# Second mixer block in float16 halves, the third block's pool groups projected in the fourth, scale sums by one product

## The chip, the cores and the metric

The kernel runs on one core of a Trainium2 chip. The metric is the device time of one execution in microseconds; three executions of the kernel before took 2219.76, 2223.6 and 2225.92 us, the median is 2223.6 us. The profile is of one more execution.

## The reference

The kernel computes one streaming step of a hybrid encoder layer for 2048 prompt tokens and 64 decode tokens, D_MODEL 1024, all inputs in float32:

```python
def hybrid_layer(x, conv_prev, s_prev, pool_prev, pos0, chunk, ...):
    h = rmsnorm(x, norm1_w)
    proj = h @ w_in                               # 1024 -> 2568 columns
    qkv_pre, z, a, b, u_pool = ...                # columns of proj
    qkv, conv_new = causal_short_conv(qkv_pre, conv_prev, conv_w)
    ...                                           # l2norm of q, k; gates g, beta from a, b
    o, s_new = gated_delta_chunked(q, k, v, g, beta, s_prev, chunk)
    o = rmsnorm(o, onorm_w) * silu(z)             # 4 heads of 128 columns
    o_pool, pool_new = multiscale_pool(u_pool, pool_prev, pos0, pool_w, pool_scale)
    x = x + concatenate([o_delta, o_pool]) @ w_out
    h = rmsnorm(x, norm2_w)
    x = x + (silu(h @ w_gate) * (h @ w_up)) @ w_down
```

The gated delta rule is a recurrence over chunks of tokens, four heads side by side. The pool group has four groups of 128 columns, each with its trailing mean of 2, 4, 8 or 16 frames.

## The kernel before

**Tiling.** The 2112 tokens are worked off as four mixer blocks: block 0 has 576 (with the 64 decode tokens), blocks 1 to 3 have 512 each. After them the FFN runs over three groups of 704 tokens by a Strassen scheme in float16 halves. In a mixer block, `project` makes 21 tiles of 128 columns: tile 0 holds the gate columns, tiles 1 to 16 the four heads (q, k, v, z for each), tiles 17 to 20 the pool groups. To keep float32 precision each factor is cut into a high and a low half, and a tile takes three products for each of its eight k (high x high, high x low, low x high), 24 matmuls; tile 0 takes 16. That is 496 matmuls for a block of 512 tokens. The output projection (`out_proj`) has 8 x 24 = 192 for each block.

**Two kinds of halves.** `J16` gives the first block that works in float16: a block with `B.f16 = j >= J16` has float16 halves, which need scales that are powers of two, from the sums of squares of a weight tile. The others have float32r halves (`wsplit`). Before, J16 is 2:
- block 0 loads each raw tile of `w_in` as two pieces (`wrp`, 256 KB each), splits it on ScalarE and VectorE, squares it on ScalarE for its scale (sums in `psq`), and stores the float32r halves to DRAM (`wsd`, in the profile `wnd`);
- block 1 loads the halves back from there;
- block 2 loads the raw tiles again, converts them to float16 halves (`convert`, `split16`: ScalarE scales and rounds the high half, VectorE takes the rest) and stores them (`w16`, in the profile `wn`);
- block 3 loads those.

The output weights go the same way, one block later: block 0's output projection runs in block 1 and prepares float32r halves, block 1's runs in block 2 and loads them back (`wod`), block 2's and 3's run behind block 3 with float16 halves, whose scales `convert` makes from squares of its own (`two_squares`, `wcwout`).

**Scales.** `scale_of` turns n columns of partial sums into one scale: VectorE copies the columns to bfloat16, TensorE multiplies each column by a constant matrix (n products of one column, summed in PSUM), and `half_power` makes a power of two from the bits in three VectorE operations. It is used for FFN weights (`ws` with 4 columns, `wd` with 2), for the FFN's activations (`ec` with 8), and for `wcwout`. `win_scales` makes the scales of all 21 tiles of `w_in` at once, at the start of block 1; `out_scale` makes those of the mixer's outputs, in block 3.

**Order.** A list `plan` names the weight tiles in the order of their use; `prep` prepares them three ahead of use. `PRE_AT` names the places in it where sums of FFN weights are prepared early. The mixer's recurrence (`Chain` objects, moved on by `pump` inside the matmul loops) runs between the wide matmuls of the projections. All operations are recorded first. A planner (`Machine.issue`) then plays the order of each engine with costs of its own, in windows of operations and with random variations, and keeps the play in which TensorE loses least. `emit` prints the winning order, so that nearly every instruction has the line of that loop, L374 before and L375 after. SP issues all DMAs.

**The third block** (`B.kept`, j = 2) is a special case: its output projection doesn't run in the next block but at the very end. Its heads' and pools' results wait in DRAM (`od`), and are loaded and split to halves behind block 3 (`od{k}`). Its pool groups (`pools(B)`) are projected at the end of block 2; the fourth block projects its own behind its last head (`LASTPOOLS`).

Of the kernel before, what the change touches and what calls it, by code (L numbers as in the profile page):

```python
# [11 lines left out]
BF16 = mybir.dt.bfloat16  # L12
# [41 lines left out]
LASTPOOLS = {3: ((0,), (1,), (2, 3))}  # L54
# [10 lines left out]
class Machine:  # L65
# [126 lines left out]
    def issue(self):  # L192
# [4 lines left out]
        while len(self.out) < len(ops):  # L197
# [3 lines left out]
            for i in range(PLAYS):  # L201
# [6 lines left out]
                self.play(stop + AFTER)  # L208
# [103 lines left out]
    def play(self, stop):  # L312

        wait, ready, total = self.wait, self.ready, self.total
        while len(self.out) < total and self.front < stop:
# [28 lines left out]
            self.out.append(op)  # L344
            for nm in op.tiles:
# [116 lines left out]
def hybrid_kernel(ctx, tc, a, o):  # L462
# [69 lines left out]
    ctx.enter_context(tc.manual_schedule())  # L532
    tc.nc.scalar.preload_act_table_set("natural_log_exp_and_others")
# [80 lines left out]
    def half_power(out, x):  # L614

        ts(out, x, TINY, None, ALU.add)
        bits = out.bitcast(mybir.dt.int32)
        ts(bits, bits, 1, 0x7F800000, ALU.logical_shift_right, ALU.bitwise_and)
        ts(bits, bits, -1.0, float(189 << 23), ALU.mult, ALU.add)

    def scale_of(out, squares, n, top, ps, tag="sqb"):

        cols = (cpool if tag == "sqb" else wq["pool"]).tile([P, 8], BF16, tag=tag, name=f"{tag}{machine.n}", bufs=2)[:, :n]
# [39 lines left out]
    for j in range(NBLK):  # L663
# [3 lines left out]
        if j < NBLK - 1:  # L667
            plan += win[:at] + ([("wout", m) for m in range(KT)] if j else []) + win[at:]
        else:
            plan += win[:1]  # L670
            for h in range(NH):
                plan += win[1 + 4 * h : 5 + 4 * h] + [win[17 + g] for gs in LASTPOOLS.get(h, ()) for g in gs]
        plan[base:] = with_pres(j, plan[base:])
    assert not pres
    plan += [("hw", "wout", m) for m in range(KT)]
    LASTO = ([(m, p) for ms in (range(6), range(6, KT)) for p in (1, 0) for m in ms])
    plan += [("wl", m, p) for m, p in LASTO]

# [41 lines left out]
    def prep():  # L720
# [13 lines left out]
        elif key in stored and key[0] in wsd:  # L734
            parts = []
            for i in range(2):
                t = wtiles(f"p{i}")[1]()
                nc.sync.dma_start(out=flat(t), in_=wsd[key[0]][key[1], i])
                parts.append(t)
# [3 lines left out]
        elif key[0] in ("win", "wout"):  # L743
            parts = []
            for i in range(2):
# [91 lines left out]
    def convert(key, t):  # L837

        _, nm, m = key
        raws = []  # L840
# [18 lines left out]

    def win_scales():  # L860

        cols = gp.tile([P, 2, 21], BF16, tag="cols", name="cols")
        nc.vector.tensor_copy(cols, psq)
        ps = psp.tile([P, 512], F32, tag="mm", name="wscales", bufs=PSM)[:, :21]
        for i in range(2):
            mm(ps, parts_b[2.0**15], cols[:, i], start=i == 0, stop=i == 1)
# [787 lines left out]

    def pools(B, groups=((0,), (1,), (2, 3))):
# [5 lines left out]
    def out_proj(B):  # L1661
        acts = [(k, B.o[k]) for k in (4, 5, 6, 7, 0, 1, 2, 3)]

        src = stream_x(a["xT"], "xc", B.t0, "xc")
        for ms in ((0, 1), *((m,) for m in range(2, KT))) if B.kept else ((m,) for m in range(KT)):
            ws = [weights("hw", "wout", m) if B.f16 else weights("wout", m) for m in ms]
            for m in ms if B.f16 else ():
# [576 lines left out]
```

## Time and profile before

| | |
|---|---|
| median of three executions | 2223.6 us |
| lowest and highest | 2219.76 and 2225.92 us |
| the profiled execution | 2219.34 us, span 2217.6 us |
| DMA | 466.41 MB, mean 210 GB/s |
| chain that ended last | PE 30%, DVE 1%, all others 0% (the rest isn't named) |

The profiled execution took 2219.34 us, of which 2217.6 us are the span from its first instruction to its last. Times in rows count from the start of that span. A row that groups instructions gives the line, engine, operation, tiles (out <- in, buffer numbers left out), shapes and count, then the busy time in us, the mean ns of one, and the idle time of the engine ahead of them with what ended it. Row names: `pp` is the PSUM tile of a projection, `pz` that of an output projection, `wsp` a tile of weight halves, `wrp` a raw weight tile, `h` and `op` the halves of the activations; names with `_p` and `_s` belong to the recurrence of the prompt and of the decode tokens. Matmuls are pipelined, so their durations overlap, and the mean duration of one is longer than the time until the next may start. A row of the timeline gives start, length, engine, line, operation, tiles and count of instructions that follow each other.

The first matmul waits 8.7 us for its weights; blocks 0 to 3 then start at 8.7, 209.2, 438.1 and 648.0 us, the last output projections at 824.6, the FFN at 928.2.

### The profile page before, as it was taken

Reading aid. Unit: us, or ns where it says so; the run is one execution under the profiler, and the core shown is the slowest. Engines: PE = TensorE matmul, PEld = TensorE weight load, DVE = VectorE, ACT = ScalarE, POOL = GpSimd, SP = SyncE. Lnnn points to the kernel's source line nnn. Section 1 sums busy time; section 2 is a strip of 40 time slices with the busy share of each in tenths; the row PEclk is TensorE's granted clock in tenths of the full one; section 3 lists DMA queues with packets and bytes.
Section 4 is the critical chain, followed back from the end, with each engine's and each line's share of the span. In section 5 each row is a group of like instructions: output and inputs, shape, how many; then the busy total and the mean of one; then the engine's idle time right before and its main releaser. Section 6 shows DMA issues by size and latency. Waiting matters only on the chain. (4 is left out here: it accounts for less than half of the span.)

```text
span 2217.6 us, 41377 instructions
## 1 busy us (share of the span) xinstructions
PE 2178.4 (98%) x14785; PEld 1535.4 (69%) x14785; DVE 1597.9 (72%) x3361; ACT 1364.6 (62%) x3235; POOL 652.4 (29%) x783
## 2 busy tenths in 40 slices
PE   8999999999999999999999999999999999999998
PEld 7999898767656666468666676666666566666667
DVE  7888785797779798688899977656543845445447
ACT  7998776787778996587666846732333343312414
POOL 3424342435335563021321117532101421100102
PEclk9999999999999999999999999999999999999999
DMA  7765577566664458996785668978545656444442
GB/s 280 245 213 172 163 269 268 174 211 230 212 216 145 143 157 285 303 333 238 232 295 205 216 204 288 341 244 265 156 143 158 201 186 220 154 145 151 140 140 72
DMA packets 222270, 466.41 MB, mean 210 GB/s; under 512 B 27504, under 2 KB 88944, under 8 KB 222064
## 3 DMA queue, kind: packets, MB, share of 16 engines
q1 hardware_dynamic: 221488, 463.06, 63.5%
q8 instruction: 115, 1.88, 0.3%
q14 instruction: 91, 0.75, 0.1%
q10 hardware_dynamic: 576, 0.72, 0.1%
HBM read 320.26 MB, written 143.43 MB: 209 GB/s over the span
## 5 line engine op out<-in xcount | busy, mean ns | idle before, releaser
L374 PE MATMUL pp<-h,wsp 128*128 128x288 f32 (+2 forms) x2480 | 517.9, 354 | 11.7 <-DVE wsp L374 10.2
L374 PEld LDWEIGHTS <-wsd 128*128 128x128 f16 x2352 | 229.7, 98 | 127.5 <-issue 6.2
L374 PEld LDWEIGHTS pp<-h,wsp 128*128 128x128 f32 x1488 | 226.8, 191 | 27.0 <-ACT wsp L374 8.7
L374 PE MATMUL dx<-hq,wsd 128*128 128x352 f16 x1232 | 233.0, 314 | 1.8 <-DVE y L374 1.5
L374 PEld LDWEIGHTS <-ws11S 128*128 128x128 f16 x1584 | 153.7, 98 | 83.0 <-ACT ws11S L374 1.5
L374 PEld LDWEIGHTS <-wsS 128*128 128x128 f16 x1584 | 154.1, 98 | 82.3 <-issue 2.0
L374 PEld LDWEIGHTS <-wsS3S 128*128 128x128 f16 x1584 | 154.3, 98 | 81.2 <-issue 0.5
L374 POOL TENSOR_TENSOR q<-hr,hr 128x352 f32<-128x352 f32 x52 | 53.9, 1036 | 444.6 <-DVE hr L374 391.2
L374 PEld LDWEIGHTS <-wsp 128*128 128x128 f16 x1184 | 109.1, 98 | 106.8 <-issue 2.7
L374 DVE SCALAR_TENSOR_TENSOR y<-dx,es,y 128x352 f32<-128x352 f32 x240 | 136.0, 580 | 63.7 <-PE dx L374 62.8
L374 ACT COPY g<-px 128x352 f32<-128x352 f32 x132 | 58.4, 443 | 190.3 <-PE px L374 188.9
L374 ACT ACTIVATE hr<-g,pscale 128x352 f32<-128x352 f32 x132 | 76.6, 586 | 143.3 <-DVE g L374 143.0
L374 PE MATMUL pz<-op,wsp 128*128 128x288 f32 (+2 forms) x768 | 158.6, 347 | 0.0
L374 PE MATMUL px<-hA,ws11S 128*128 128x352 f16 x792 | 139.2, 313 | 0.3 <-DVE ws11S L374 0.2
L374 PE MATMUL py<-hA,ws11S 128*128 128x352 f16 x792 | 137.9, 313 | 0.9 <-ACT ws11S L374 0.9
L374 PE MATMUL pz<-hA,wsS 128*128 128x352 f16 x792 | 136.5, 312 | 0.0
L374 PE MATMUL py<-hA,wsS3S 128*128 128x352 f16 x792 | 134.4, 312 | 0.3 <-ACT u L374 0.3
L374 PE MATMUL px<-hA,wsS 128*128 128x352 f16 x792 | 130.8, 312 | 1.4 <-ACT g L374 1.3
L374 PE MATMUL px<-hB,ws 128*128 128x352 f16 x792 | 130.2, 312 | 1.1 <-DVE u L374 0.9
L374 PE MATMUL px<-hA,wsS3S 128*128 128x352 f16 x792 | 130.6, 313 | 0.0
L374 PE MATMUL dy<-hq,wsd 128*128 128x352 f16 x672 | 124.9, 313 | 3.0 <-ACT hq L374 2.3
L374 ACT CAST TV_p<-pt_p 128x512 f16<-128x512 f32 x192 | 110.0, 586 | 23.3 <-PE pt_p L374 20.2
(797 smaller groups left out, 4838.6 us busy)
## 6 DMA issues: line engine op xcount, KB each, us to landing
ws11S<-g SPq DMA_DIRECT2D x44, 512.0 KB, 3.8
wsS<-g SPq DMA_DIRECT2D x44, 512.0 KB, 3.6
wsS3S<-g SPq DMA_DIRECT2D x44, 512.0 KB, 3.6
wrp<-in_win_dram SPq DMA_DIRECT2D x84, 256.0 KB, 3.5
wnd<-wsp SPq DMA_DIRECT2D x42, 512.0 KB, 4.9
wsp<-wnd SPq DMA_DIRECT2D x42, 512.0 KB, 4.0
wsd<-dn SPq DMA_DIRECT2D x40, 512.0 KB, 3.6
xd<-x2d SPq DMA_DIRECT2D x96, 176.0 KB, 3.9
```

The costliest lines, as they stand in the source:

```text
L374: getattr(getattr(self.nc, op.eng), name)(*args, **kw)
```

## The change

It has four parts.

1. **J16 from 2 to 1.** Block 1 and its output projection (which runs in block 2) work in float16 halves. `convert` now runs for block 1's tiles, in blocks 0 and 1; blocks 2 and 3 load the float16 halves. The float32r stores and reloads (`wnd`, `wod`) are gone. Block 0's output projection stays in float32r. `win_scales` runs ahead of the first conversion instead of at the start of block 1, and `out_scale` in block 1 instead of block 3.
2. **Scales of the output weights** come from squares that are taken when block 0's float32r halves of them are prepared (16 pieces, in block 1), all eight at once (`wout_scales`, with `tile_sums`), instead of from `two_squares` and `scale_of` in each `convert`. Their inverse is multiplied with the output scale once.
3. **The third block's pool groups** are projected in block 3, behind the fourth block's heads, with the same weight tiles as the fourth block's own (`pools_of(prev, B)`): for each group 24 matmuls of block 2, then 24 of block 3. So the last output projection of the third block takes its k in the order 0 to 7, heads first.
4. **`scale_of`** sums the n columns on VectorE (`tensor_reduce`) and makes one product of one column. `half_power` has two operations instead of three.

Beside these, `es` gets three buffers, `PRE_AT` has other places, and the planner gives up a play that is already worse than the best (which changes no winner).

```diff
-LASTPOOLS = {3: ((0,), (1,), (2, 3))}
...
     def half_power(out, x):
-        ts(out, x, TINY, None, ALU.add)
         bits = out.bitcast(mybir.dt.int32)
-        ts(bits, bits, 1, 0x7F800000, ALU.logical_shift_right, ALU.bitwise_and)
+        ts(bits, x.bitcast(mybir.dt.int32), 1, 0x7F800000, ALU.logical_shift_right, ALU.bitwise_and)
         ts(bits, bits, -1.0, float(189 << 23), ALU.mult, ALU.add)
...
     def scale_of(out, squares, n, top, ps, tag="sqb"):
-        nc.vector.tensor_copy(cols, squares[:, :n])
-        for i in range(n):
-            mm(ps[:, :1], parts_b[top], cols[:, i : i + 1], start=i == 0, stop=i == n - 1)
+        nc.vector.tensor_reduce(out=cols, in_=squares[:, :n], op=ALU.add, axis=mybir.AxisListType.X)
+        mm(ps[:, :1], parts_b[top], cols, start=True, stop=True)
         half_power(out, ps[:, :1])
...
-            plan += win[:at] + ([("wout", m) for m in range(KT)] if j else []) + win[at:]
+            if j == NBLK - 2:
+                win = win[:17]
+            plan += win[:at] + ([("hw", "wout", m) if j > J16 else ("wout", m) for m in range(KT)] if j else []) + win[at:]
...
-        elif key in stored and key[0] in wsd:
-            parts = []
-            for i in range(2):
-                t = wtiles(f"p{i}")[1]()
-                nc.sync.dma_start(out=flat(t), in_=wsd[key[0]][key[1], i])
-                parts.append(t)
...
-                if key[0] == "win":
+                if len(key) == 2:
                     act(raw, raw, AF.Square, accum_out=psq[:, i, key[1] : key[1] + 1])
                 parts.append(t)
-            if len(key) == 2:
-                due.append((key, [(wsd[key[0]][key[1], i], t) for i, t in enumerate(parts)]))
...
     def convert(key, t):
         _, nm, m = key
+        if m == 0:
+            (win_scales if nm == "win" else wout_scales)()
...
-        if nm == "win":
-            scale = pscale[:, 0, m : m + 1]
-        else:
-            sq = two_squares(f"c{nm}{m}", *raws, t[:, 1, 1].bitcast(BF16))
-            scale, inv = (pscale[:, j, 21 + m : 22 + m] for j in range(2))
-            scale_of(scale, sq, 2, 2.0**15, psp.tile([P, 512], F32, tag="mm", name=f"wc{nm}{m}", bufs=PSM))
-            nc.vector.reciprocal(inv, scale)
+        m0 = 0 if nm == "win" else 21
+        scale = pscale[:, 0, m0 + m : m0 + m + 1]
...
+    def wout_scales():
+        half_power(pscale[:, 0, 21:], tile_sums(KT, "wo"))
+        nc.vector.reciprocal(oinv, pscale[:, 0, 21:])
+        ts(oinv, oinv, oscale[:, 5:], None, ALU.mult)
...
+    def pools_of(*blocks):
+        for g in range(4):
+            w = weights("hw", "win", 17 + g)
+            for B in blocks:
+                ps = psmm(f"pp{B.j}_{17 + g}_0")
+                for k in range(KT):
+                    one_k(B, 17 + g, w[k // 4], ps[:, : B.NB], k, slice(0, B.NB))
+                    pump()
+                B.pools.append(Chain(pool_group(B, g, [ps])))
...
-        acts = [(k, B.o[k]) for k in (4, 5, 6, 7, 0, 1, 2, 3)]
+        acts = [(k, B.o[k]) for k in (range(KT) if B.kept else (4, 5, 6, 7, 0, 1, 2, 3))]
...
-        if j == NBLK - 1:
+        if j == J16:
             out_scale()
-        if j == 1:
-            win_scales()
...
-            if nxt is None and h in LASTPOOLS:
-                pools(B, LASTPOOLS[h])
+            if nxt is None and h == NH - 1:
+                pools_of(prev, B)
...
         if nxt is not None:
-            pools(B)
+            if not B.kept:
+                pools(B)
...
-PRE_AT = {1:(4,8,12,16,20),2:(4,7,10,13,16,19),3:(3,6,9,12,15)}
+PRE_AT = {1: (4, 8, 12, 16, 20), 2: (4, 7, 10, 13, 14, 16), 3: (3, 7, 11), 4: (3, 5)}
...
-J16 = 2
+J16 = 1
```

What the planner makes of it stands in the order of the engines. In its names the number behind the letters is the block, and the next ones tell the tile: `pp1_9_0` is tile 9 of block 1, `wsp` its weights, `pz0_7` the output projection of block 0, and `pk`, `po`, `Gam`, `vn` belong to the recurrence.

TensorE in block 1, tile 9, before:

```order
L374 MATMUL pp1_9_0_1273<-h0_1_839,wsp0_53_1206 128x512 x6
L374 MATMUL pp1_9_0_1273<-h1_1_840,wsp1_53_1207 128x512
L374 MATMUL pk1_p1_1_1_1315<-vn1_p1_1_1_1327,ktl_p1_1_1_1084 128x128
L374 MATMUL po_p1_1__1274<-Gam_p1_1_1_1135,vn1_p1_1_1_1327 128x128
L374 MATMUL pp1_9_0_1273<-h1_1_840,wsp1_53_1207 128x512 x2
L374 MATMUL pz0_7_288_1259<-op0_0_219,wsp0_51_1176 128x288 x12
```

The same place now:

```order
L375 MATMUL pk0_p1_1_0_1296<-rhs0_p1_1_0_1297,X_p1_1_0_1245 128x128
L375 MATMUL po_p1_1__1293<-Qd_p1_1_0_1096,Sp_207 128x128
L375 LDWEIGHTS onesb_101
L375 MATMUL wd4_2_1085<-sqb3464_1086,onesb_101 128x1
L375 MATMUL pz0_7_288_1278<-op0_0_219,wsp0_51_1192 128x288 x7
L375 LDWEIGHTS wsp_53_1222
L375 MATMUL pp1_9_0_1292<-h_1_844,wsp_53_1222 128x512
L375 LDWEIGHTS Wh_p1_1_1_1175
L375 MATMUL pf_p1_1_1_1274<-TV06_p1_1_1_1265,Wh_p1_1_1_1175 128x128
```

A float32r matmul stands in the list without a weight load; each float16 one has an instruction of its own for it ahead. The scale product `wd` stands alone where it was one of two.

ScalarE at the seam of blocks 0 and 1, from the operation that ends `win_scales`' sums (`wscales` before), before:

```order
L374 ACTIVATE psq_107,oscale_106<-wscales_895 128x4 x2
L374 CAST Wh_p0_3_1_753<-Gst_p0_3_1_745 128x256
L374 CAST Wh_s0_755<-Gst_s0_733 128x256
L374 ACTIVATE vn0_p0_2_1_758<-pk0_p0_2_1_756,kn_p0_2_1_533 128x128
L374 CAST h0_1_839<-xb0_576_841 128x512
```

The same place now, where the sums are called `wiscales`:

```order
L375 ACTIVATE psq_107,oscale_106<-wiscales_736 128x4 x2
L375 CAST hi_p0_2__822<-osq_p0_2__805 128x512
L375 CAST TV11_p0_3_1_780<-pt1_p0_3_1_787 128x512
L375 ACTIVATE wsp_22_734<-wrp0_22_737,pscale_105 128x4x64 x2
L375 ACTIVATE qsq_p0_3__935<-Yqk0_3_559 128x512
L375 ACTIVATE wsp_22_734<-wrp1_22_738,pscale_105 128x4x64
L375 ACTIVATE osq_p0_2__805<-os_p0_2__821,qeps_99 128x512
L375 CAST TV11_s0_789<-pt1_s0_796 128x512
```

The conversions of block 1's tile 0 (`wsp_22`) stand between operations of block 0's recurrence now. ScalarE's conversions of 128x512 from `wrp` to float16 numbered 0, 11, 33 and 16 in blocks 0 to 3, and number 10, 34, 16 and 0 now.

ScalarE where the third block's first pool groups are read out of PSUM (`pe2_0`, `pe2_1`), at the end of block 2 before:

```order
L374 ACTIVATE pe2_0_2074<-pp2_17_0_2057,pscale_105 128x512
L374 CAST TV06_p2_2_1_2122<-pt6_p2_2_1_2129 128x512
L374 ACTIVATE wsp_99_2032<-wrp1_99_2034,pscale_105 128x512
L374 ACTIVATE E1_2_3_2051<-E1_2_3_2051 128x512
L374 ACTIVATE TV1F_p2_2_1_2137<-TV32F_p2_2_1_2136 128x256
L374 ACTIVATE pe2_1_2103<-pp2_18_0_2073,pscale_105 128x512
```

Now these stand at the end of block 3, each followed by the fourth block's own group (`pe3_0`):

```order
L375 ACTIVATE pe2_0_2669<-pp2_17_0_2644,pscale_105 128x512
L375 ACTIVATE Yvz3_3_2540<-ext3_11_2590,consts_95 128x512
L375 CAST TV11_p3_2_0_2601<-pt1_p3_2_0_2610 128x512
L375 ACTIVATE YtF_p3_1_0_2606<-px_p3_1_0_2605 128x256
L375 ACTIVATE YtF_p3_1_1_2609<-px_p3_1_1_2608 128x256
L375 ACTIVATE E1_3_3_2640<-Yqk3_3_2539 128x512
L375 ACTIVATE E1_3_3_2640<-E1_3_3_2640,onec_98 128x512
L375 ACTIVATE E1_3_3_2640<-E1_3_3_2640 128x512
L375 CAST TV02_p3_2_0_2624<-pt2_p3_2_0_2631 128x512
L375 ACTIVATE pe3_0_2703<-pp3_17_0_2660,pscale_105 128x512
```

The recurrence around them is now that of the fourth block (`p3`) instead of the third (`p2`), and no conversion of weights stands between them.

More of the change, by code (lines that the diff above doesn't have):

```diff
@@ L344, in play @@
             self.out.append(op)
+            if limit is not None and self.free["tensor"] - self.work >= limit:
+                return
             for nm in op.tiles:
@@ L532, in hybrid_kernel @@
     ctx.enter_context(tc.manual_schedule())
+    ctx.enter_context(tc.nc.allow_low_precision(reason="sums of squares that choose a power of two"))
     tc.nc.scalar.preload_act_table_set("natural_log_exp_and_others")
@@ L858, in convert, with tile_sums, win_scales @@
         due.append((key, [(w16[nm][m], t.rearrange("p i q n -> p (i q n)"))]))
[L860 to L864, printed above, removed]
+    def tile_sums(n, name):
+        cols = gp.tile([P, 2, 21], BF16, tag="cols", name=f"cols{name}")[:, :, :n]
+        nc.vector.tensor_copy(cols, psq[:, :, :n])
+        ps = psp.tile([P, 512], F32, tag="mm", name=f"{name}scales", bufs=PSM)[:, :n]
         for i in range(2):
             mm(ps, parts_b[2.0**15], cols[:, i], start=i == 0, stop=i == 1)
+        return ps
+    def wout_scales():
+        half_power(pscale[:, 0, 21:], tile_sums(KT, "wo"))
+        nc.vector.reciprocal(oinv, pscale[:, 0, 21:])
+        ts(oinv, oinv, oscale[:, 5:], None, ALU.mult)
+    def win_scales():
+        ps = tile_sums(21, "wi")
         for i, lo, step in ((0, 4, 4), (1, 17, 1)):
@@ L1666, in out_proj @@
             ws = [weights("hw", "wout", m) if B.f16 else weights("wout", m) for m in ms]
-            for m in ms if B.f16 else ():
-                ts(oinv[:, m : m + 1], oinv[:, m : m + 1], oscale[:, 5:], None, ALU.mult)
             for lo, n in B.subs:
@@ L1812, in hybrid_kernel @@
     machine.boost = ODB
-    for k in (4, 5, 6, 7, 0, 1, 2, 3):
+    for k in range(KT):
         t = wpool.tile([P, 512], F32, tag="xc", name=f"od{k}", bufs=XBUFS["xc"])
```

18 lines of the change are left out of this document (9 added, 9 removed).

## The prediction

> **What bounds the kernel now.** I first read the totals on the page (busy time, share of the span and instructions of each engine), then the busy time by stage. The six stretches start where each stage's first projection matmuls stand: blocks 0, 1, 2 and 3, the last output projections, and the FFN. A row gives the stretch, its length, busy time (instructions) of PE, PEld, DVE, ACT and POOL, the granted clock, the DMA engines' share and GB/s.
>
> ```profile
> PE 2178.4 (98%) x14785; PEld 1535.4 (69%) x14785; DVE 1597.9 (72%) x3361; ACT 1364.6 (62%) x3235; POOL 652.4 (29%) x783
> ```
> ```profile
> 8.70:209.20 200.50, 197.17 (x1566) 185.56 (x1567) 175.25 (x390) 180.81 (x495) 78.22 (x109) 1.00 0.67 224
> 209.20:438.10 228.90, 228.02 (x1558) 195.80 (x1557) 165.54 (x364) 168.66 (x408) 80.84 (x114) 1.00 0.67 221
> 438.10:648.00 209.90, 206.77 (x1275) 133.96 (x1275) 176.33 (x357) 171.95 (x409) 84.21 (x110) 1.00 0.66 217
> 648.00:824.60 176.60, 170.84 (x1171) 105.29 (x1170) 147.97 (x340) 155.09 (x394) 98.80 (x132) 1.00 0.51 156
> 824.60:928.20 103.60, 103.38 (x616) 56.84 (x614) 77.50 (x175) 61.19 (x144) 25.60 (x26) 1.00 0.84 278
> 928.20:2217.60 1289.40, 1272.18 (x8608) 857.91 (x8607) 851.85 (x1722) 622.05 (x1380) 282.23 (x286) 1.00 0.63 207
> ```
>
> TensorE is busy 98% of the span and its clock is granted in full in every stage. The length of a stretch less TensorE's busy time is its idle time: 3.3 us in block 0, 0.9 in block 1, 3.1 in block 2, 5.8 in block 3, 0.2 in the tail and 17 in the FFN. So the time is TensorE's queue, and an edit is worth what it takes out of that queue, less any new idle time. ScalarE and VectorE are loaded to 70 to 90% in blocks 0 to 2, which is where they could become late.
>
> **Term A: 688 matmuls go from float32r to float16.** These are the second block's 496 wide projection matmuls and the 192 wide ones of its output projection.
>
> ```profile
> L374 PE MATMUL pp<-h,wsp 128*128 128x512 f16 x992 | 237.1, 379 | 2.0 <-DVE wsp L374 1.5 <-DVE h L374 0.3
> L374 PE MATMUL pp<-h,wsp 128*128 128x512 f32 x496 | 128.9, 401 | 0.0
> L374 PE MATMUL pz<-op,wsp 128*128 128x512 f32 x192 | 52.4, 406 | 0.0
> L374 PE MATMUL pz<-op,wsp 128*128 128x512 f16 x192 | 46.5, 379 | 0.0
> ```
>
> The mean durations overlap each other in the pipeline, so I take busy time per matmul: 128.9/496 = 260 ns against 237.1/992 = 239 ns, and 52.4/192 = 273 against 46.5/192 = 242. By these rows the change is worth 496 x 0.021 + 192 x 0.031 = 10.4 + 5.9 = 16.3 us. That is the upper bound, because a busy time also holds the pipeline's fill and drain at each switch to another operation. What one matmul adds to the queue is read from the timeline, from one row's start to the next row's:
>
> ```profile
> 363.50 15.67 PE L374 MATMUL pp<-h,wsp 128*128 128x512 f32 x68
> 379.01 0.60 PE L374 MATMUL ptk_p<-consts,Yqk 128*128 128x128 f32 x4
> ...
> 635.11 2.97 PE L374 MATMUL pp<-h,wsp 128*128 128x512 f16 x13
> 637.92 0.22 PE L374 MATMUL px_p<-TV_p,TV1F_p 128*128 128x128 f16 x1
> ...
> 398.04 0.28 PE L374 MATMUL py_p<-TV_p,Wh_p 128*128 128x128 f16 x2
> 398.12 2.09 PE L374 MATMUL pp<-h,wsp 128*128 128x512 f32 x8
> 400.05 0.23 PE L374 MATMUL py_p<-TV_p,Wh_p 128*128 128x128 f16 x1
> 400.12 0.28 PE L374 MATMUL pt_p<-Yt_p,TV_p 128*128 128x128 f16 x2
> 400.23 0.28 PE L374 MATMUL pt_p<-TV_p,Yt_p 128*128 128x128 f16 x2
> ```
>
> 68 float32r matmuls take 379.01 - 363.50 = 15.51 us, 228 ns each; 13 float16 ones 2.81 us, 216 ns each. In long runs the step is 12 ns, and 688 x 12 ns = 8.3 us, the lower bound. The third piece shows why it is more: a run of 8 that follows a narrow float16 pair takes 1.93 us, 0.20 us over 8 x 0.216, where the long run's price gives 0.10. The pair ahead of it takes 0.08 us; the pair behind it takes 0.11 (400.12 to 400.23), so 0.03 is given back, and each such switch costs some 0.075 us that float16 doesn't pay. I count 57 runs of this kind; the first and the last:
>
> ```profile
> 210.55 1.41 PE L374 MATMUL pp<-h,wsp 128*128 128x512 f32 x5
> 211.80 0.38 PE L374 MATMUL po_p__703<-Gam_p,vn_p 128*128 128x128 f32 x2
> ...
> 567.31 1.17 PE L374 MATMUL pz<-op,wsp 128*128 128x512 f32 x4
> 568.32 0.40 PE L374 MATMUL os_p__1908<-hi_p__1909,ones 128*128 128x512 f32 x1
> ```
>
> Their excess over 216 ns is 1.25 - 1.08 = 0.17 and 1.01 - 0.86 = 0.15 us, of the same size. So 8.3 + 57 x 0.075 = **12.6 us**, between 8.3 and 16.3.
>
> A float16 matmul has a weight load of its own, and the other rows to weigh are these:
>
> ```profile
> L374 PEld LDWEIGHTS pp<-h,wsp 128*128 128x128 f32 x1488 | 226.8, 191 | 27.0 <-ACT wsp L374 8.7 <-DVE h L374 1.1 <-issue 0.9
> L374 PEld LDWEIGHTS <-wsp 128*128 128x128 f16 x1184 | 109.1, 98 | 106.8 <-issue 2.7 <-DVE wsp L374 2.0
> ```
>
> Both kinds load 128 columns per matmul, 191 ns in float32r and 98 ns in float16, and both are shorter than the matmul that they can hide behind. The Trainium skill, "TensorE: Matmul & The Clock Gate", section "The mechanism", says that a weight load overlaps running matmuls only where it targets other rows of the array. All loads here cover 128 rows, so by that rule 688 x 98 ns = 67 us would stand open after the change; the 13 float16 matmuls at 216 ns, each with its load, contradict it.
>
> **Term B: 199 products of one column go.** The scales of power-of-two halves were made by n products of one column each, now by one sum on VectorE and one product. By the instruction lists of the two kernels there were 112 (`ec`), 88 (`ws`), 44 (`wd`) and 16 (`wcwout`), of which 15, 22, 22 and 0 stay, and two products of 8 columns come in: 260 - 59 - 2 = 199.
>
> ```profile
> L374 PE MATMUL ec<-sqe,onesb 128*128 128x1 bf16 x112 | 4.9, 164 | 0.0
> 1071.56 0.34 PE L374 MATMUL ec<-sqe,onesb 128*128 128x1 bf16 x8
> 1071.76 1.35 PE L374 MATMUL py<-hA,wsS3S 128*128 128x352 f16 x8
> ```
>
> Eight of them hold the queue for 0.20 us, 25 ns each: **5.0 us**. By busy time it is 0.34/8 = 42 ns, so 8.5 us at most, and nothing at least, where the next wide matmul would have waited anyway. The same page's section "Wait — 56ns, not 53.3ns?" gives some 62 ns for a small matmul when its decoding is done in software, by which these would be 12 us; the 25 ns of the row are the floor that it gives for decoding in hardware. VectorE has one operation for another here and one less in each scale, off the path.
>
> **What lies beside other work, at 0.** The conversions to float16 move forward by a block.
>
> ```profile
> L374 ACT ACTIVATE wsp<-wrp,pscale 128x512 f16<-128x512 f32 x56 | 39.0, 719 | 5.1 <-PE pp L374 2.7 <-DVE pscale L374 1.7 <-PE pz L374 0.4
> L374 ACT ACTIVATE wrp<-wrp 128x512 f32<-128x512 f32 x42 | 26.5, 632 | 0.9 <-DVE wsp L374 0.9
> L374 ACT ACTIVATION_READ_ACCUMULATOR wrp<-wrp 128x1 f32 x42 | 8.3, 197 | 0.0
> L374 DVE SCALAR_TENSOR_TENSOR wsp<-wrp,pscale,wsp 128x512 f16<-128x512 f32 x56 | 43.7, 794 | 5.4 <-ACT wsp L374 5.1
> ```
>
> ScalarE's conversions stood 0, 11, 33 and 16 in the four blocks and stand 10, 34, 16 and 0 after. Block 0 gets 10 x 0.719 = 7.2 us: 180.8 + 7.2 = 188 of 200.5 us. Block 1 gets 23 x 0.719 and the 16 squares of the output weights at 0.632 + 0.197: 29.8 us, 168.7 + 29.8 = 198.5 of the 219.8 us left of it (228.9 less 496/688 of term A). VectorE has 165.5 + 23 x 0.794 = 184 there. Both fit, with 12 us to spare in block 0 and 21 in block 1, and conversions run three tiles ahead of their use. The scales of all 21 tiles now have to be there at the seam of blocks 0 and 1: a square, a sum, two operations on bits, then one conversion pair, some 4 us, behind three tiles of 24 products that take over 15 us. If this cover were gone, the first tile would wait the 4 us. So 0, between 0 and 37 for everything uncovered; of these ends I take the near one, by the rows of block 1, where TensorE waited 0.9 us.
>
> The stores and reloads of split weights go.
>
> ```profile
> wnd<-wsp SPq DMA_DIRECT2D x42, 512.0 KB, 4.9
> wsp<-wnd SPq DMA_DIRECT2D x42, 512.0 KB, 4.0
> ```
>
> SP issues all DMAs in order, and it issues 91 fewer; the 17 more loads of float16 weights for block 2 replace raw loads. TensorE waited for none of these (below), with the engines of the DMA busy to 0.66: 0 gained, at most the 3.1 us idle in block 2.
>
> The third block's pool groups: 4 x 24 matmuls leave the end of block 2 and run beside the fourth's own, so their matmuls cost 96 x 0.216 = 20.7 us in either place. Their old place was filler for the recurrence around the seam at 648, where the waits of block 3 are:
>
> ```profile
> PE pk_p L374 <- DVE Sp L374: 2.0, 2, 1.7
> PE pp L374 <- DVE wsp L374: 1.5, 1, 1.5
> ```
>
> These are 3.5 of its 5.8 us. New is that the last of these groups must go through its pool chain to DRAM and back (`od`) before the third block's last output projection, two transfers of 4 to 5 us by the rows above and some six operations of 0.7 to 0.8 us: 13 us as an estimate. Over it lie the 24 matmuls of the fourth block's own last group (5.2 us) and what is left of its recurrence: a wait of 0 to 8. Against it stands the idle time in blocks 2 and 3, of which up to 8.9 us could go. I take 0 net, between -8.9 and +20.7, since the idle rows of the stage are single waits under 2 us.
>
> **Sum.** 12.6 + 5.0 = 17.6 us off the profiled execution's 2219.34 us gives 2201.7. The median of the runs stands 4.26 us above that execution; I carry the same saving to it: 2223.6 - 17.6 = **2206.0 us**.
>
> **Rivals.**
> 1. More is gained (2190): the busy rows are the true price and the idle time of blocks 2 and 3 goes: 16.3 + 8.5 + 8.9 = 33.7 us. For it: blocks 2 and 3 lose their conversions. Against: the starts in the timeline. Chance 0.12.
> 2. No change (2217 to 2227, about 2222): the filler is missing between blocks 2 and 3, and TensorE idles there for 11 to 20.7 us. For it: ScalarE and VectorE are at 82 and 84% in block 2, and the recurrence is a chain of narrow steps. Against: the fourth block brings 496 filler matmuls of its own, and the waits found are single ones under 2 us. Chance 0.11.
> 3. Slower (2240): ScalarE works in order, so conversions and squares queue ahead of steps of the recurrence, for which TensorE waits. If 34 of the 37 us in blocks 0 and 1 come uncovered, 2206 + 34 = 2240; it decides from 24 us uncovered (2230.3). For it: 94% load in block 0. Against: conversions before did the same in block 2 at 82% with 3.1 us of idle. Chance 0.06.
> 4. The change doesn't speed a matmul up, since each float16 load stands open: 98 ns on 688 matmuls, 2206 + 67 = 2273. Against it is the run of 13. The skill's rule under term A would give this. Chance 0.02.
>
> **How the numbers follow.** The forecast (2197 to 2214) has 0.69. Forecast and rival 1 end more than 0.3% (6.7 us, about what a measurement can tell from no change) below 2223.6: 0.81 faster. Rival 2 is within: 0.11. Rivals 3 and 4: 0.08 slower. The range for 8 in 10 goes from 2193, halfway into rival 1, to 2218, the near end of rival 2.
>
> **What would show it.** Right: the second block's wide matmuls appear as f16 at about 239 ns busy each, its stage is 8 to 10 us shorter, block 2 (with the output projection) 3 to 5, the FFN 3 to 5, and one-column products number 59. Wrong: waits of TensorE for ScalarE's `TV_p` or `ktl_p` in blocks 0 and 1 (rival 3), idle of over 10 us between blocks 2 and 3 or before the last output projections (rival 2), or float16 runs in block 1 at over 230 ns (rival 4). The forecast also fails if the newly planned order of the FFN, whose 17 us of idle I leave as they are, comes out worse by as much.

## The result and the profile after

The changed kernel took 2200.37 us (median of four executions, 2198.21 to 2202.24), against 2222.78 us before: ratio 0.9901, 95% interval 0.9885 to 0.9917, so 22 us less. A second set of executions on another occasion gave 0.9903 (0.9887 to 0.9919). The forecast was 2206.0 us in a range of 2193 to 2218. The profiled execution took 2198.21 us, 21.1 us less than the one of before.

Busy time by stage, with the columns of the prediction (blocks 0 to 3, the last output projections, the FFN; where two blocks' tiles overlap, the second's tile 1 opens its stage):

```profile
8.80:219.40 210.60, 202.56 (x1612) 188.44 (x1612) 181.18 (x409) 190.86 (x521) 80.74 (x112) 1.00 0.34 106
219.40:437.80 218.40, 215.74 (x1467) 150.48 (x1466) 190.30 (x394) 189.09 (x456) 79.38 (x105) 1.00 0.62 203
437.80:622.50 184.70, 181.81 (x1183) 109.71 (x1182) 146.11 (x305) 146.76 (x351) 81.72 (x111) 1.00 0.53 173
622.50:823.10 200.60, 199.27 (x1392) 125.33 (x1391) 167.19 (x347) 165.89 (x425) 112.36 (x146) 1.00 0.45 137
823.10:917.60 94.50, 94.06 (x497) 48.23 (x496) 54.40 (x112) 42.80 (x99) 14.02 (x15) 1.00 0.82 262
917.60:2196.40 1278.80, 1264.14 (x8441) 853.00 (x8441) 843.14 (x1675) 622.22 (x1379) 281.23 (x286) 1.00 0.63 207
```

Idle time (length less TensorE's busy time) is now 8.0, 2.7, 2.9, 1.3, 0.4 and 14.7 us, against 3.3, 0.9, 3.1, 5.8, 0.2 and 17.2 before. The third block's pool groups lengthen stage 4 and shorten stage 3. The groups that the change touches:

```profile
L375 PE MATMUL pp<-h,wsp 128*128 128x512 f16 x1488 | 357.4, 379 | 1.1 <-ACT pe L375 0.7 <-DVE wsp L375 0.4
L375 PE MATMUL pz<-op,wsp 128*128 128x512 f16 x384 | 92.2, 379 | 0.5 <-DVE xc L375 0.2 <-DVE op L375 0.2
L375 PE MATMUL wd<-sqb,onesb 128*128 128x1 bf16 x22 | 3.7, 167 | 0.3 <-DVE xc L375 0.3
L375 PE MATMUL ws<-sqb,onesb 128*128 128x1 bf16 x22 | 3.6, 168 | 0.0
L375 PE MATMUL ec<-sqe,onesb 128*128 128x1 bf16 x15 | 2.5, 167 | 0.0
```

All wide products of blocks 1 to 3 are float16 now, at 357.4/1488 = 240 ns of busy time, and 59 products of one column are left. To see what the queue holds, I summed the time from each matmul's start to the next one's start over the two traces, by kind. A sum holds the waits that follow each kind too (the narrow float16 ones include 33 in bfloat16):

```
us, start to next start                        before   after
wide, 512 columns, float32r and float16         468.6   449.1
wide, 288 columns (block 0), float32r           198.4   199.1
narrow, float16                                  94.5   100.4
narrow, float32                                 136.2   137.2
all others of the mixer                          22.9    23.1
mixer and output projections                    920.6   908.8
FFN, products of one column                       5.3     1.4
FFN, all others                                1274.7  1268.9
```

So 11.8 us come from the mixer and 9.7 from the FFN, of which 3.9 are small products and 5.8 are not. That last figure was in no term of the sum.

### The profile page after: what moved, and what is told of

It reads as the page before. It is cut to its first block, busy times and chain, and to the rows that moved or that the text cites. A ratio compares the mean times of both kernels' runs of the same rounds, so it can differ in the third digit from the quotient of the medians.

```text
span 2196.4 us, 40706 instructions
## 1 busy us (share of the span) xinstructions
PE 2157.6 (98%) x14586; PEld 1475.3 (67%) x14586; DVE 1585.8 (72%) x3255; ACT 1362.5 (62%) x3235; POOL 651.9 (30%) x783
## 5 line engine op out<-in xcount | busy, mean ns | idle before, releaser
L375 PE MATMUL pp<-h,wsp 128*128 128x512 f16 (+1 forms) x2480 | 510.3, 349 | 14.1 <-DVE wsp L375 11.0
L375 PEld LDWEIGHTS <-wsp 128*128 128x128 f16 x1872 | 173.2, 98 | 168.4 <-issue 6.4
L375 PE MATMUL pz<-op,wsp 128*128 128x288 f32 (+1 forms) x768 | 152.1, 341 | 0.6 <-DVE xc L375 0.2
L375 PEld LDWEIGHTS pp<-h,wsp 128*128 128x128 f32 x992 | 137.6, 191 | 15.8 <-ACT wsp L375 8.7
```

The costliest lines, as they stand in the source:

```text
L375: getattr(getattr(self.nc, op.eng), name)(*args, **kw)
```

## The experiments

The three theories are: prices alone (each kind of matmul holds TensorE's queue for its own time, idle time comes out even); the pool groups' new place; and the order, which the planner draws anew for every kernel by random variations. Float16, the products and the pool groups were each made alone on the kernel before; the products and the pool groups were also undone alone in the changed kernel, float16 wasn't. Then the planner's seed was changed. Two small things of the change ride along: the third `es` buffer is in every kernel but before, before_seed2 and pools_alone, and the new places of `PRE_AT` are in every kernel with the second block in float16. Every time below stands beside before on the same chip.

| run | us | before, same chip | ratio and interval |
|---|---|---|---|
| products_alone | 2213.53 | 2223.31 | 0.9954 (0.9937 to 0.9970) |
| f16_alone | 2211.43 | 2223.31 | 0.9946 (0.9933 to 0.9960) |
| pools_alone | 2232.35 | 2223.31 | 1.0041 (1.0028 to 1.0055) |
| before_seed2 | 2220.45 | 2223.31 | 0.9985 (0.9977 to 0.9994) |
| after_again | 2200.00 | 2221.44 | 0.9903 (0.9887 to 0.9919) |
| after_seed2 | 2198.91 | 2221.44 | 0.9900 (0.9885 to 0.9915) |
| pools_back | 2197.10 | 2221.44 | 0.9893 (0.9879 to 0.9907) |
| products_back | 2209.96 | 2221.44 | 0.9954 (0.9941 to 0.9967) |
| products_alone_seed2 | 2198.72 | 2223.41 | 0.9893 (0.9877 to 0.9909) |
| products_back_seed2 | 2206.85 | 2223.41 | 0.9924 (0.9911 to 0.9936) |
| f16_alone_seed2 | 2204.97 | 2223.41 | 0.9917 (0.9904 to 0.9931) |
| pools_back_seed2 | 2202.28 | 2223.41 | 0.9904 (0.9890 to 0.9917) |

### One product for each scale, alone and undone

In the kernel before, `scale_of` and `half_power` as in the change and nothing else of it, with the third `es` buffer:

```diff
-        for i in range(n):
-            mm(ps[:, :1], parts_b[top], cols[:, i : i + 1], start=i == 0, stop=i == n - 1)
+        nc.vector.tensor_reduce(out=cols, in_=squares[:, :n], op=ALU.add, axis=mybir.AxisListType.X)
+        mm(ps[:, :1], parts_b[top], cols, start=True, stop=True)
```

> The kernel before with the fourth part alone (one sum on VectorE and one product of one column instead of n, two operations for the power of two instead of three): 260 small products become 75, 185 fewer. Queue theory (each holds TensorE's queue for its 25 ns): 4.6 us less than before, 2218.2 by the median of 2222.8. Rival, they cost their busy time of 42 ns: 7.9 us less. Rival, the next wide matmul waited for its weights anyway: no change. Rival, the newly drawn order decides: anything within 5 us of before, and idle time of TensorE in the FFN that differs from 17 us by as much as the time does.

Measured: 9.8 us less. `products_back` is the same edit backwards, in the changed kernel:

> The changed kernel with its fourth part undone: n products of one column for each scale again, three operations for the power of two. 183 products more. Queue theory at 25 ns: 4.6 us above the changed kernel, 2205. At their busy time: 7.7 us, 2208. If the fourth part also shortened the chain of scales that the FFN waits for: 10 us, 2210, with idle time in the FFN 4 us longer.

Measured: 10.0 us above the changed kernel. Both are twice the price. The price itself is right: in the timeline the product of one column after the change holds the queue for 0.03 us, and the wide one behind it starts as if nothing had been there (start, us, engine, line, operation, tiles, count):

```profile
1706.94 0.17 PE L375 MATMUL ec<-sqe,onesb 128*128 128x1 bf16 x1
1706.97 0.61 PE L375 MATMUL dx<-hq,wsd 128*128 128x352 f16 x3
1707.41 0.46 PE L375 MATMUL dy<-hq,wsd 128*128 128x352 f16 x2
```

The neighbours lose nothing either: 16 matmuls around eight products took their usual time and 0.20 us more, those around one product 0.025 us more. So the rest lies elsewhere, and the traces of all runs show where. The mixer is counted from the first matmul to the first of the FFN, the FFN from there to the last matmul's start (us):

| kernel | `es` buffers | products | mixer | FFN |
|---|---|---|---|---|
| before | 2 | n | 920.6 | 1279.9 |
| before_seed2 | 2 | n | 921.8 | 1277.2 |
| pools_alone | 2 | n | 931.5 | 1284.9 |
| f16_alone | 3 | n | 915.9 | 1273.9 |
| products_back | 3 | n | 915.0 | 1274.9 |
| f16_alone_seed2 | 3 | n | 910.0 | 1274.2 |
| products_back_seed2 | 3 | n | 912.3 | 1274.6 |
| products_alone | 3 | one | 927.6 | 1266.9 |
| products_alone_seed2 | 3 | one | 911.9 | 1266.6 |
| the changed kernel, twice | 3 | one | 908.8, 909.6 | 1270.3, 1271.4 |
| after_seed2 | 3 | one | 915.9 | 1266.0 |
| pools_back | 3 | one | 907.8 | 1269.1 |
| pools_back_seed2 | 3 | one | 917.5 | 1266.5 |

The FFN falls into three groups that don't overlap: two buffers and n products (mean 1280.7), three buffers and n products (1274.4), three buffers and one product (1268.1). So the fourth part itself shortens the FFN by 6.3 us, of which 3.9 are the products, and the kernels with a third `es` buffer are shorter by another 6.3. The new `PRE_AT`, which the four of the middle group have too, isn't needed for it: products_alone has the old one and lies with the other kernels of its group. `products_alone` has both, 13.1 us in the FFN, and its newly drawn mixer takes 7.0 back. `products_back` against `after_again` is 3.5 us longer in the FFN and 5.4 in the mixer: it met the expectation of 10 us, but not the reason given for it, 4 us more of idle time in the FFN.

The waits of ScalarE in the FFN show the rest of the chain (waiter, releaser, us in total, times, longest); first before, then the changed kernel:

```profile
ACT hq L374 <- DVE es L374: 27.6, 11, 4.6
```
```profile
ACT hq L375 <- DVE es L375: 14.5, 8, 2.5
```

ScalarE waits for `es`, the scale of the FFN's hidden activations, 27.6 us before and 14.5 after. In the seven profiles with n products it is 17.1 to 27.6 us with a longest wait of 2.8 to 8.7; in those with one product 13.6 to 18.2 us, and the longest wait is 2.5 each time. In the trace of before, one scale comes late, that of the tenth of fifteen hidden groups (first its products on TensorE, then VectorE):

```profile
1721.65 0.34 PE L374 MATMUL ec<-sqe,onesb 128*128 128x1 bf16 x8
```
```profile
1744.53 0.15 DVE L374 TENSOR_SCALAR es<-ec 128x1 f32<-128x1 f32 x1
1744.71 0.34 DVE L374 TENSOR_SCALAR es<-es 128x1 int32<-128x1 int32 x2
1744.97 0.57 DVE L374 SCALAR_TENSOR_TENSOR y<-dx,es,y 128x352 f32<-128x352 f32 x1
1745.46 0.15 DVE L374 RECIPROCAL es<-es 128x1 f32<-128x1 f32 x1
```

In f16_alone, also with n products, the scale of the same group follows its products at once:

```profile
1717.97 0.34 PE L377 MATMUL ec<-sqe,onesb 128*128 128x1 bf16 x8
```
```profile
1718.35 0.16 DVE L377 TENSOR_SCALAR es<-ec 128x1 f32<-128x1 f32 x1 [0.30 <-PE ec L377]
```

And so it does in the changed kernel, one operation shorter, behind the product at 1706.94 above:

```profile
1707.15 0.16 DVE L375 TENSOR_SCALAR es<-ec 128x1 int32<-128x1 int32 x1
1707.34 0.15 DVE L375 TENSOR_SCALAR es<-es 128x1 int32<-128x1 int32 x1
1707.53 0.16 DVE L375 RECIPROCAL es<-es 128x1 f32<-128x1 f32 x1
```

From the products' end to the scale's start it is 22.5 us before, 26.8 in before_seed2 and 21.0 in pools_alone, the three kernels with two `es` buffers; VectorE works off 28 to 39 additions to `y` in between, which read older scales. In the eleven profiles with three buffers it is under 0.1 us. Behind the late scale TensorE stands idle; this is before (idle time ahead and its releaser in brackets):

```profile
1747.66 0.61 PE L374 MATMUL dy<-hq,wsd 128*128 128x352 f16 x3
1750.58 0.31 PE L374 MATMUL dy<-hq,wsd 128*128 128x352 f16 x1 [2.31 <-ACT hq L374]
1751.60 0.74 PE L374 MATMUL dy<-hq,wsd 128*128 128x352 f16 x2 [0.71 <-DVE hq L374]
1753.58 0.75 PE L374 MATMUL dx<-hq,wsd 128*128 128x352 f16 x2 [1.24 <-DVE y L374]
```

In the 14 us behind this scale's start TensorE's waits sum to 4.3 us before, 3.6 in before_seed2 and 4.2 in pools_alone, against 0.7 to 1.1 in the other eleven. And these 4.3 us cost more than themselves. The stretches below give TensorE's busy time (instructions), its granted clock, the DMA share and GB/s:

```profile
1740.00:1748.00 8.00, 8.00 (x56) 1.00 0.59 188
1748.00:1751.00 3.00, 0.58 (x3) 1.00 0.84 235
1751.00:1757.00 6.00, 4.16 (x14) 0.50 0.69 211
1757.00:1765.00 8.00, 8.00 (x52) 0.95 0.75 232
```

The granted clock falls to 0.50 after the gap and stays there until 1757.8. The changed kernel has no such stretch ahead of its end. No run changes the buffers alone. But f16_alone and products_alone have, of the whole change, only the third buffer in common, and neither has the late scale. So it is the buffer, named in passing beside the four parts, that takes this stall away, and not the shorter chain: that one goes from 0.73 to 0.54 us, from its first operation to the end of the reciprocal, where nothing stands between.

### Float16 alone

The first two parts of the change, with the new places of `PRE_AT` and the third `es` buffer; `pools`, `LASTPOOLS`, `scale_of` and `half_power` stay as they were.

```diff
-J16 = 2
+J16 = 1
```

> The first and second part of the change alone (second block and its output projection in float16, output weights' squares gathered early); the scale sums by n products and the third block's pool groups are as before. Queue theory: the wide matmuls give 12.6 to 16.3 us and the 16 products that go with the output weights' own scales 0.4, so 13 to 17 us less than before, 2206 to 2210; 688 fewer float32r matmuls show as about 239 ns busy each instead of 260 to 273. Rival, the pool groups' move carries part of the gain: less than 12 us. Rival, ScalarE's earlier conversions cost idle time: TensorE idles 5 us or more longer in blocks 0 and 1 than the 4.2 us of before, whether or not the pool groups move.

Measured: 11.9 us less, one below the low end of the expectation. That the number is close to the price is in part a coincidence: of the 9.5 us between the profiled executions, by the table above, 6.0 lie in the FFN, where no matmul changes its type and the third `es` buffer works, and only 4.7 in the mixer; the first matmul starts 1.3 later. The mixer's wide matmuls do go from 231 to 216 ns in the middle (start to next start), but something is given back, and the timelines show where. Before, float32r:

```profile
379.45 0.39 PE L374 MATMUL pk_p<-Sp,Yqk 128*128 128x128 f32 x2
379.59 1.17 PE L374 MATMUL pp<-h,wsp 128*128 128x512 f32 x4
```

After, float16, at a like place of block 1:

```profile
369.06 0.39 PE L375 MATMUL pk_p<-rhs_p,X_p 128*128 128x128 f32 x2
369.28 2.11 PE L375 MATMUL pp<-h,wsp 128*128 128x512 f16 x9
371.22 0.38 PE L375 MATMUL pk_p<-vn_p,ktl_p 128*128 128x128 f32 x2
371.44 0.28 PE L375 MATMUL po_p__1293<-Gam_p,vn_p 128*128 128x128 f32 x1
```

A narrow float32 pair of the recurrence held the queue for 0.14 us ahead of a float32r product and holds it for 0.22 us ahead of a float16 one: in float32r the last of the pair takes 31 ns, in float16 112. The float32r product behind it pays that back, with 314 ns (the median over all traces) instead of the 230 inside a run. Behind a narrow float16 matmul it takes 314 ns too, but only 28 of the narrow one's 56 are saved, and the narrow one behind the run takes 10 more: 66 ns for such a switch beyond the run's price, where the prediction took 75. Behind narrow float32 it is 84 less 81, next to nothing.

To price the change of type with the order held as it is before, I gave each of the 688 products and each of its neighbours the median time of its kind between its two neighbours' kinds, over all traces, once with a float32r product there and once with a float16 one. The change of type is then worth 12.8 us: the wide ones give 17.9, the float32 matmuls beside them take 3.6 back, the narrow float16 ones 0.9, and small shares of others the rest. For the other four kernels with a float32r second block it is 12.7 to 13.8, and other groupings and means give 12.1 to 14.0.

What the mixer shows is less, since idle time comes with it. In the first 429 us from the first matmul, about blocks 0 and 1, TensorE idles 9.4 to 12.1 us in the nine profiles with the second block in float16 and 3.8 to 6.7 in the five without it; in f16_alone it is 10.0 against 4.1 before. So the rival of 5 us or more in blocks 0 and 1 holds beside the price. The mixer is 912.5 us long in the mean of the nine and 922.7 in the mean of the five. What else f16_alone lost of its price in the mixer lies in its new order and isn't assigned.

### The pool groups alone and undone

In the kernel before, the third block's groups move to the fourth:

```diff
-        if nxt is not None:
-            pools(B)
+        if nxt is not None:
+            if not B.kept:
+                pools(B)
...
-            if nxt is None and h in LASTPOOLS:
-                pools(B, LASTPOOLS[h])
+            if nxt is None and h == NH - 1:
+                pools_of(prev, B)
```

> The kernel before with the third part alone: the third block's four pool groups projected in the fourth behind its heads, with shared weight tiles. It issues the same matmuls, so the queue theory gives the change of idle time alone: within 4 us of before (2219 to 2227). If the fourth block's idle time goes because of the move, its 5.8 us fall to 1 or 2 and the time is 4 us shorter. Rival, the filler is missing at the end of the third block: 5 to 20 us of idle time there, 2228 to 2243.

Measured: 9.0 us more than before. The loss isn't at the end of the third block, where the rival had it, but behind the fourth (same columns as the stretches above):

```profile
840.00:849.00 9.00, 8.72 (x61) 1.00 0.46 157
849.00:854.00 5.00, 2.67 (x18) 1.00 0.89 279
854.00:867.00 13.00, 11.26 (x43) 0.51 0.51 163
867.00:880.00 13.00, 12.99 (x69) 0.96 0.56 177
```

From 849.4 to 863.4 there is no wide product left beside the fourth block's recurrence; its narrow steps wait for ScalarE and VectorE in turn, and the granted clock is 0.50 from 854.3 to 867.9. The profiled execution was the slowest of six (2236.89 us): its mixer is 10.9 us longer than before's, and its FFN 4.9, with the late scale and a half clock behind it again. In the tail stand 3.9 us of waits (849 to 868 us) and by estimate at most 6.8 lost at the half clock, half of 13.7. In the changed kernel, the move undone:

> The changed kernel with its third part undone: the third block's pool groups projected at the end of the third block again, the fourth block's own behind its last head in three groups. If the move costs what it cost alone (9 us): 2191. If it is worth nothing beside the other parts: 2200. If the move fills the idle time of the fourth block (1.3 us in the changed kernel, 5.8 before): about 2204 with some 4 us of idle time back in that block.

Measured: 2.9 us less than the changed kernel in the same batch, with intervals that overlap. The move is worth nothing there that could be told. Its loss alone lies mostly in that tail. `after_seed2` has a smaller one at the same place, a wait of 3.4 us with 3.4 us at half clock behind it; the other kernels with the move have no wait over 1.2 us there.

### Another draw of the order

The seed of the planner's random variations:

```diff
-        rand, stop = random.Random(1), 0
+        rand, stop = random.Random(2), 0
```

> The kernel before with another seed of the planner's random variations and nothing else: the same instructions in another order. Queue theory: within 3 us of before, all of it in idle time. Rival, the order decides as much as the prices: 5 us or more to either side.

> The changed kernel itself, on the same chip as the next three. As measured: about 22 us less than before.

> The changed kernel with another seed of the planner's random variations and nothing else. Queue theory: prices stay, within 4 us of the changed kernel (2196 to 2205). Rival, the order that the change happened to draw holds part of its gain: 6 us or more above it, all of it as idle time of TensorE.

Measured: before_seed2 2.9 us less than before and after_seed2 1.1 us less than the changed kernel, so for these two the draw is small. It isn't for others:

> The fourth part alone on the kernel before, both with the planner's second seed: to be held against before with that seed, whose ratio to before was 0.9985 (2220.45 us). If the fourth part is worth 5 us by price and the other 5 us of the first pair were the draw: 2213 to 2218, with no fixed sign to what goes beyond 5. If it is worth 10 whatever the draw: 2210.

> The changed kernel without its fourth part, with the planner's second seed: to be held against the changed kernel with that seed (2198.9 us, ratio 0.9900). Price theory with a draw: 2204 give or take 4. Ten us whatever the draw: 2209. In the records, stretches at a granted clock of 0.5 should stand behind every longer piece of idle time of TensorE, and the run's excess over 5 us should be those.

> The first and second part alone, with the planner's second seed: against before with that seed (2220.45 us). Price theory: 12.6 to 16.3 us less, 2204 to 2208, give or take 4 for the draw. Rival, the first pair's 11.9 us is all that there is: 2208 to 2209.

> The changed kernel without its third part, with the planner's second seed: against the changed kernel with that seed (2198.9 us). If the pool groups' place is worth nothing but the draw: 2195 to 2203. If their old place is better, as with the first seed (2.9 us): 2196. This kernel is also the candidate for one that beats both; against the changed kernel it has to be clear of the interval.

Measured: `products_alone_seed2` is 24.7 us faster than before without a single float16 matmul more, as fast as the whole change; both of its expectations missed, by 11 us and more. 13.6 of the 24.7 us (by the ratios) lie between it and the same kernel with the first seed: its mixer is 911.9 us long from start to start instead of 927.6, and no stretch ahead of its end has a lowered clock, where the first seed's has 3.4 us of waiting for `vn_p` and 6.8 us at a clock of 0.50 behind it. The other expectations held: `products_back_seed2` 2206.85 (between 2204 and 2209), `f16_alone_seed2` 2204.97 (2204 to 2208), `pools_back_seed2` 2202.28 (within 2195 to 2203). The long stretches at 0.50 that were expected of `products_back_seed2` aren't there. No version beats the changed kernel clearly: pools_back, products_alone_seed2 and the changed kernel lie at 0.9893, 0.9893 and 0.9903, with intervals of 0.0016 to either side at most.

By pairs that differ in one part, at the same seed (ratios times 2222 us; in the pairs with a star the third `es` buffer differs too, so that the mean is of the others; in all pairs of float16 `PRE_AT` does):

| part | seed 1 | seed 2 | mean without stars |
|---|---|---|---|
| one product | -10.2*, -11.3, -11.8 | -20.4*, -5.3, -2.9 | -7.8 |
| float16 | -12.0*, -13.6 | -15.1*, +2.4 | -5.6 |
| pool groups | +9.1, +2.2, +1.8 | -0.9, +1.6 | +2.8 |

A difference of two of these ratios is good to some 5 us. The spread in the row of float16 is 16 us; -20.4 and +2.4 share one run, `products_alone_seed2`. What a part gives in one pair is its price plus a draw of some 5 to 10 us, and one pair is no measure of it.

## Why the prediction was right, step by step

- **What bounds the kernel**: right. TensorE is still busy 98% of its span, and both terms came out of its queue. Of the signs named for it, the 239 ns (240) and the 59 products are there; block 1's stage is 10.5 us shorter (8 to 10 were named), block 2's 4.5 beside the 20.7 of the pool groups (3 to 5). The FFN is 9.7 us shorter instead of 3 to 5, and that block 0's stage would be 10.1 us longer and the last output projections' 9.1 shorter was in no sign.
- **Term A** (12.6 us): right. With the order held, the price is 12.8 us. The step inside a run is a little more than 12 ns (230 to 216), the switch a little less than 75 ns (66). The wide part alone (17.9 us) is above the 16.3 of the busy rows, so that was no upper bound for it; the neighbours bring the sum back under it.
- **Term B** (5.0 us): right. The small products hold 3.9 us less of the queue in the FFN, and 38 fewer of them at 25 ns give about 1 us in the mixer. Beyond the price, the fourth part shortens the FFN by 2.4 us at three buffers; which wait that is, isn't settled.
- **"What lies beside other work, at 0"**: wrong by 2.0 us in sum, and near 0 only because its parts have both signs. Blocks 0 and 1 idle 10.7 us now, against 4.2; block 3 idles 1.3 against 5.8. The first comes with float16, in all nine profiles. That is rival 3's place at less than a fifth of its price. TensorE's longest waits in block 0 of the changed kernel are for VectorE (the 8.8 in the first row is the start):

```profile
PE pp L375 <- DVE wsp L375: 10.6, 2, 8.8
PE pt_p L375 <- DVE Yt_p L375: 2.4, 3, 1.5
```

So a late ScalarE isn't shown. Whether VectorE's conversions do it wasn't tried.

- **The pool groups at 0**: right in the changed kernel, where their place can't be told from the other. The tail that rival 2 feared came in pools_alone and, smaller, in after_seed2, among the last output projections.
- **The FFN's 17 us "as I leave them"**: wrong, and this is where the step from 17.6 to some 22 us lies. The FFN gave 5.8 us more than its products. The stall behind the late scale, 4.3 us of waits and 6.8 at half clock, is what before has there and the changed kernel hasn't. The third `es` buffer, which takes it away, stands in the remark beside the four parts, and the prediction gave it no term.
- **Rivals**: rival 1 had the direction of the surplus but put it into blocks 2 and 3; rivals 2 and 4 fell (float16 products with loads of their own run at 216 ns).

In sum, 12.6 and 5.0 as forecast, 5.8 more from the FFN and 2.0 less from the mixer's idle time make 21.4 us, against 21.1 between the two profiled executions. The two terms were understood. That the total came as close was partly luck: one small thing went unpriced, new idle time offset a third of it, and the order drawn could have moved the time by 5 to 10 us either way.

## What to carry to other kernels

Price a change of type by the whole queue, from start to next start, neighbours included: what the narrow matmul ahead saves at a switch, the wide one behind it can pay back. Where an engine is at 98%, look up what its longest stalls wait for and which buffer holds that up; here a third buffer for a tile of six columns went with as much of the FFN's time as the whole fourth part. Read every run by stage, since a total can agree with a price while half of it comes from elsewhere, as in f16_alone. And where a planner draws the order, hold each part against more than one draw before crediting it.

## What the runs showed of the hardware

Short stalls in the middle of full work can halve the granted clock for longer than they last. Before, 2.31 us of idle time and two shorter gaps brought 6.8 us at 0.50; in pools_alone 5 us at half load brought 13.7. Yet 3.05 us in one piece brought nothing in the changed kernel:

```profile
1360.00:1369.00 9.00, 9.00 (x62) 1.00 0.79 263
1369.00:1372.00 3.00, 0.13 (x1) 1.00 0.24 90
1372.00:1380.00 8.00, 7.82 (x54) 1.00 0.87 302
```

The clock's own record in the traces shows more of it. In each of the 14 profiles the changes of the granted clock lie whole multiples of 3.413 us apart, to within 4 ns, and the half-clock stretches ahead of the end last 3.4, 6.8 or 13.7 us. So in these runs the clock changes only on a grid of 3.41 us. I took TensorE's busy share in each stretch of that grid. The stretches at full clock that were followed by a half clock, ahead of the end, are nine, busy to between 0.19 and 0.77; the one before is 0.29 (1747.6 to 1751.0). Every stretch under 0.40 was followed by a half clock; from 0.42 to 0.77 both happen, so that no sharp threshold comes out. From half clock, it came back only after stretches busy to 0.99 or more. The changed kernel's gap of 3.05 us lies across two stretches, 0.66 and 0.45, and neither was enough. The stall behind the late scale fell on 0.55 and 0.48 in before_seed2 and kept its full clock there, where before it fell on 0.29. So where a stall lies on the grid bears on whether it costs only itself.

The Trainium skill, "TensorE: Matmul & The Clock Gate", section "HAM oscillation — how this bites in real kernels", has as its rule that gaps of TensorE over some 3.4 us are to be avoided. The last trace agrees with it (3.05 us, no loss); the first doesn't quite, since there no single gap was longer than 2.31 us. By the grid, several gaps in one stretch count together.
